# One-hot matrices of eight tokens in two VectorE instructions instead of four, residual loads and output gathers paced

## The chip, the cores and the metric

The kernel runs on one core of a Trainium2 chip. The metric is the device time of one execution in microseconds, here the median of three runs. TensorE multiplies 128x128 tiles, VectorE (DVE), ScalarE (ACT) and GpSimd (POOL) work on 128 partitions; SyncE (SP) and others issue DMAs.

## What is computed

Two layers of a trunk over 256 context rows and 512 latent rows of 1024 numbers. Each layer has a mixer (attention and a short convolution in layer 0, an mLSTM in layer 1) and then PEER, a layer of 16384 experts. PEER picks 16 experts for each token and each of 8 heads, and adds up their output rows:

```python
def block(xb):
    q = (xb @ w_q).reshape(PEER_BLOCK, PEER_HEADS, 2, PEER_DHALF)
    s = jnp.einsum('thpd,hpkd->thpk', q, subkeys).astype(jnp.float32)
    s1, i1 = lax.top_k(s[:, :, 0], PEER_TOPK)
    s2, i2 = lax.top_k(s[:, :, 1], PEER_TOPK)
    cand = (s1[..., :, None] + s2[..., None, :]).reshape(...)
    cidx = (i1[..., :, None] * PEER_NKEYS + i2[..., None, :]).reshape(...)
    top, pos = lax.top_k(cand, PEER_TOPK)
    idx = jnp.take_along_axis(cidx, pos, axis=-1)
    g = jax.nn.softmax(top, axis=-1)
    ue, ve = u[idx], v[idx]
    act = jax.nn.gelu(jnp.einsum('td,thkd->thk', xb, ue), approximate=False)
    return jnp.einsum('thk,thkd->td', g * act, ve)
```

The result is RMSNorm of the latent stream after layer 1.

## The kernel before

The span falls into stages: mixer of layer 0 (to about 485 us), peer_u of layer 0 (U0, to 1536), peer_v0 (V0, from 1579 to about 2290), mixer of layer 1 (to about 2670), peer_u of layer 1 (U1, to 3447), peer_v1 (V1, to the end).

Most blocks of 128 tokens ("dense" ones) don't gather expert rows. For them U multiplies all 16384 expert rows, 128 chunks of 128, by the tokens: a chunk is loaded (uf, L997), split into a high part by ScalarE (uh, L109) and a low part by VectorE (ul, L112), multiplied in three terms on TensorE (aps, L681), and put through Gelu by ScalarE (ga, L1024), which is stored to DRAM (gad). The routing weight of each expert pair is made as a matrix per token: over 128 (head, choice) pairs, a one-hot matrix of the first key index times a one-hot matrix of the second, the latter weighted by the softmax (in a high and a low part). V then multiplies gad by that weight (gf, read from gd) and by the output rows of all experts.

The one-hot matrices are made by `prep(t0)` for eight tokens: an iota tile is compared with the tokens' indices (L862 for the first index, L863 for the second), and the second is multiplied by the two parts of the weight (L865, twice). `gbuild(t0, g)` takes four of the eight tokens: for each, two matmuls of 128x128 (gps, L879), stationary from the first matrix, moving from the second; ScalarE copies the result to stg (L881), which is stored to gd. There are four dense blocks in U0 and three in U1, with 16 preps each.

The other blocks (two in layer 0, one in layer 1) are gathered by rows: POOL gathers urows (L922), VectorE takes a dot product (L928); in V, POOL gathers vrows (L1094) and VectorE adds them up (`v_add`: L1100, L1102).

What VectorE and TensorE do beside the chunks is laid out by a planner in peer_u: four queues (routing, the one-hot matrices with their matmuls, dot products, background work), each item with a weight in microseconds; in each chunk items are handed out until a share of the total weight is spent, from the queue that lags most. The scheduler of the language then orders the instructions of each engine; `tc.issue_after(x)` keeps what is in its block behind instruction x in the order. The gps matmuls stand on TensorE between the matmuls of the chunks.

In V, `v_chunk` loads a chunk of output rows (vf, L1063, on SP's queue), with gaf and gf (L1066, L1070), splits them and multiplies gaf by gf (L1083); TensorE adds up in acc (L1125 in V0, L1191 in V1), with matmuls that stand four chunks behind the loads. `finish` of V0 loads the residual rows vht (L1131) on POOL's queue; V1 loads fg (the last norm's gains, L1174, on SP's queue) and four vht (L1183, on POOL's) at its start.

Of the kernel before, what the change touches and what calls it, by code (L numbers as in the profile page):

```python
# [10 lines left out]
F32 = mybir.dt.float32  # L11
F32R = mybir.dt.float32r
F16 = mybir.dt.float16
# [3 lines left out]
ALU = mybir.AluOpType  # L17
# [4 lines left out]
P = 128  # L22
D = 1024
# [20 lines left out]
PH = 8  # L44
# [13 lines left out]
QS = 2  # L58
# [9 lines left out]
def row_bcast(ap, n):  # L68
    return bass.AP(tensor=ap.tensor, offset=ap.offset, ap=[[0, P], [1, n]])
# [3 lines left out]
def kernel(ctx: ExitStack, tc: tile.TileContext, a: dict, out: bass.AP, dbg=None, stop=None):  # L73
    nc = tc.nc
    dbg = dbg or {}
    vec, act, pe, pool = nc.vector, nc.scalar, nc.tensor, nc.gpsimd
# [575 lines left out]
    def peer_u(layer, tiles):  # L652
# [12 lines left out]
        with ExitStack() as s1:  # L665
# [101 lines left out]
            def stage2(t):  # L767
                H = 2 if t < ng else 4
                keep = t >= ng
                d = {}  # L770
# [81 lines left out]
                def prep(t0):  # L852
                    def f():
                        def col(q):
                            return d["it"][:, q, None, t0:t0 + 8].rearrange("p o (g t) -> p g o t", t=4) \
                                .to_broadcast([P, 2, P, 4])

                        io = GP[1][:, None].to_broadcast([P, 2, P, 4])
                        p1 = GP[0].tile([P, 2, P, 4], F16, name="p1", bufs=2)
                        p2 = [GP[0].tile([P, 2, P, 4], F16, name=f"p2{q}", bufs=2) for q in range(2)]  # L860
                        eq = GP[0].tile([P, 2, P, 4], F16, name="p2e", bufs=1)
                        vec.tensor_tensor(p1, io, col(0), op=ALU.is_equal)  # L862
                        vec.tensor_tensor(eq, io, col(1), op=ALU.is_equal)  # L863
                        for q in range(2):
                            vec.tensor_tensor(p2[q], eq, col(2 + q), op=ALU.mult)  # L865
                        d[t0] = p1, p2
                    return f

                def gbuild(t0, g):
                    def f():  # L870
                        t1 = t0 + 4 * g
                        o = t1 % 32
                        if o == 0:
                            d["stg"] = GP[0].tile([P, P, 32], F32, name="stg", bufs=2)
                        gp = pp.tile([P, 512], F32, name="gps", bufs=2)
                        p1, p2 = d[t0]
                        for i in range(4):
                            for q in range(2):
                                pe.matmul(gp[:, i * P:(i + 1) * P], p1[:, g, :, i], p2[q][:, g, :, i],  # L879
                                          start=q == 0, stop=q == 1)  # L880
                        act.mul(d["stg"][:, :, o:o + 4], gp.rearrange("p (t j) -> p j t", j=P), 1.0 / GSCALE)  # L881
                        if o == 28:
                            stores.extend((t - ng, t1 // 32, d["stg"], j) for j in range(0, P, P // GS))
                        elif stores and o % 8 == 0:
                            store()
                            if o == 24:
                                while stores:
                                    store()
                    return f
# [45 lines left out]
            GP = []  # L935

            def swap():
                sq.close()
                PK["gst"].close()
                gp = mkpool(PK["st"], f"gp{layer}", side="right")  # L940
                io = gp.tile([P, P, 4], F16, name="iota")
                pool.iota(io, pattern=[[1, P], [0, 4]], base=0, channel_multiplier=0,
                          allow_small_or_imprecise_dtypes=True)
                GP.extend((gp, io))

# [6 lines left out]
            one = heads[0]  # L952
            for t in range(ng, n):
                nxt = heads[t + 1 - ng] if t + 1 < n else []
                one.append((st2[t][2], 1.0, 0))
                for pf, g0, g1 in st2[t][3]:
                    one.append((pf, 2.75, 2 * PH * QS + 1))
                    for gf in (g0, g1):
                        pend.append(gf)
                        if len(pend) > 3:  # L960
                            one.append((pend.pop(0), 0.0, 0))
                        if nxt:
                            one.append(nxt.pop(0))
                one += nxt
# [46 lines left out]
            for c in range(128):  # L1011
# [17 lines left out]
                if c == 2 * PH * QS + 1:  # L1029
                    swap()  # L1030
# [11 lines left out]
                while True:  # L1042
# [3 lines left out]
                    q = max(ok, key=lambda q: lag(q, c))  # L1046
                    f, w, _ = queues[q].pop(0)
# [39 lines left out]
        return vh, vl, wh, wl  # L1087

    def v_add(y, n, vp, accs, fetched, VB):
        for x in range(VB) if y == 0 else (y + VB - 1,):  # L1090
            if x < n * P:
                i, k = x % n, x // n
                r = fetched[x] = vp.tile([P, D], F32, name="vrows", bufs=VB)
                nc.gpsimd.indirect_dma_start(  # L1094
                    out=r, out_offset=None, in_=a["v_t"].rearrange("l c k d -> (l c k) d"),
                    in_offset=bass.IndirectOffsetOnAxis(ap=GW["row"][i][:, k:k + 1], axis=0))
        i, k = y % n, y // n
        r, gw, acc = fetched.pop(y), GW["w"][i], accs[i]
        if k == 0:
            vec.tensor_scalar(acc, r, gw[:, 0:1], None, op0=ALU.mult)  # L1100
        else:
            vec.scalar_tensor_tensor(acc, r, gw[:, k:k + 1], acc, op0=ALU.mult, op1=ALU.add)  # L1102

    def peer_v0(gd, gad, src, dst):
        G = 4
        g, n = NG[0], NT - NG[0]
        TD = n * P
        with ExitStack() as st:
            ap_ = mkpool(RT["st"], "va0", side="right")
            vp = mkpool(st, "vp0")  # L1110
# [3 lines left out]
            state, fetched, chs, added = RT["state"], {}, {}, 0  # L1114
# [13 lines left out]
            def finish(t):  # L1128
                nonlocal last
                ht = ap_.tile([P, D], F32, name="vht", bufs=2)  # L1130
                nc.gpsimd.dma_start(ht, src[t])  # L1131
                gr = grow[1 if t < 2 else 0]
                if t < g:
                    vec.tensor_tensor(accs[t], accs[t], gr, op=ALU.mult)
                else:
                    for hf in range(2):
                        hs = slice(hf * 512, (hf + 1) * 512)
                        vec.tensor_tensor(accs[t][:, hs], acc[t - g][hf], gr[:, hs], op=ALU.mult)
                vec.tensor_tensor(accs[t], accs[t], ht, op=ALU.add)
                if t >= 2:  # L1140
                    nc.gpsimd.dma_start(dst[t], accs[t])
                rs = norm_stat(accs[t], vp, vp.tile([P, D], BF16, name="vjunk"))
                if last:
                    vec.tensor_scalar(accs[last[0]], accs[last[0]], last[1], None, op0=ALU.mult)
                last = (t, rs)
# [22 lines left out]
    def peer_v1(gd, gad, src):  # L1168
        G = 4
        with ExitStack() as st:  # L1170
            vp = mkpool(st, "vp1")
            pp = mkpsum(st, "vps1")
            fg = vp.tile([P, D], F32, name="fg")
            nc.sync.dma_start(fg, row_bcast(a["norm_f"], D))  # L1174
            acc = [[pp.tile([P, 512], F32, name=f"acc{i}_{hf}") for hf in range(2)] for i in range(3)]
            accg = vp.tile([P, D], F32, name="accg")
            fetched = {}
            TD = NLAT - P
            state = V1["state"]
            hts = []  # L1180
            for i in range(4):
                ht = vp.tile([P, D], F32, name=f"vht{i}")
                nc.gpsimd.dma_start(ht, src[2 + i])  # L1183
                hts.append(ht)

            def mm(c, i, ch):
                vh, vl, wh, wl = ch
# [14 lines left out]
                        v_add(k, 1, vp, [accg], fetched, VB1)  # L1202
            for c in range(128 - G + 1, 128):
                chs[c] = v_chunk(1, vp, vp, c, gd, gad, TD, state, G + 1, (VFB, GAB, 2))
            for i in range(-1, 3):
                ht = hts[i + 1]
                if i < 0:
                    parts = accg[:, :512], accg[:, 512:]
                else:
                    parts = acc[i]  # L1210
                    for c in range(128 - G, 128):
                        mm(c, i, chs[c])
                for hf in range(2):
                    hs = slice(hf * 512, (hf + 1) * 512)
                    tmp = vp.tile([P, 512], F32, name="vtmp", bufs=2)
                    vec.tensor_tensor(tmp, parts[hf], grow[0][:, hs], op=ALU.mult)
                    vec.tensor_tensor(ht[:, hs], ht[:, hs], tmp, op=ALU.add)
                ss = vp.tile([P, 1], F32, name="fss", bufs=2)
                junk = vp.tile([P, D], BF16, name="fjunk")
                act.activation(junk, ht, AF.Square, accum_out=ss)  # L1220
                rs = rstd(ss, vp, 1.0 / D)
                vec.scalar_tensor_tensor(ht, ht, rs, fg, op0=ALU.mult, op1=ALU.mult)
                nc.sync.dma_start(out[(i + 1) * P:(i + 2) * P, :], ht)
# [461 lines left out]
```

## Time and profile before

| | us |
|---|---|
| median of three runs (lowest to highest) | 3993.28 (3991.39 to 3998.4) |
| profiled execution | 4000.77 |
| its span | 3998.9 |
| TensorE busy | 3749.9 |
| VectorE busy | 3214.4 |
| ScalarE busy | 1502.1 |
| POOL busy | 1307.3 |

The mean granted clock of TensorE is 0.972 of full speed. The profile is of one execution, 7.5 us above the median; 1.9 us of its time lie outside the span. A busy share is an average over stages with different limits. PE is a matmul, PEld a weight load.

### The profile page before, as it was taken

What the parts mean: (1) busy time and instruction counts of PE and PEld (TensorE: products, weight loads), DVE (VectorE), ACT (ScalarE), POOL (GpSimd) and SP (SyncE); (2) the same over time, 40 slices, a digit from 0 to 9 for tenths busy, and PEclk for the clock granted to TensorE, in tenths of its full rate; (3) what the DMA queues carried; (4) which work ended last, traced back from release to release, by engine and by line L of the source; (5) the groups of instructions that cost most, each with busy time, mean ns of one, the idle gap of its engine ahead of it and who ended that gap; (6) DMA issues with size and microseconds to landing.
All of it is one profiled execution on the core that took longest, in us unless ns stands there. A gap on an engine that the chain in (4) does not pass through costs nothing. (4 is left out here: it accounts for less than half of the span.)

```text
span 3998.9 us, 54009 instructions
## 1 busy us (share of the span) xinstructions
PE 3749.9 (94%) x19201; PEld 3205.2 (80%) x19201; DVE 3214.4 (80%) x6734; ACT 1502.1 (38%) x2429; POOL 1307.3 (33%) x962
## 2 busy tenths in 40 slices
PE   6988899999999995999999899888999999899998
PEld 5776688887877774888888689777899999788887
DVE  7766599999989987888898854457988877688887
ACT  4355423334333332222223365543334343333333
POOL 1521203123443334766666312213112222332221
PEclk9999999999999997999999999989999999999999
DMA  7301366468999999999999721146558888899995
GB/s 245 103 6 45 134 200 224 162 203 293 332 334 338 378 360 360 388 391 389 389 390 389 259 65 44 38 165 221 183 165 278 305 300 301 320 388 355 360 360 210
DMA packets 411663, 1036.52 MB, mean 259 GB/s; under 512 B 35584, under 2 KB 170240, under 8 KB 411392
## 3 DMA queue, kind: packets, MB, share of 16 engines
q1 hardware_dynamic: 261920, 498.69, 35.8%
q0 software_dynamic: 114336, 416.34, 28.7%
q10 hardware_dynamic: 35136, 118.05, 7.6%
q8 instruction: 150, 2.46, 0.2%
q14 instruction: 121, 0.99, 0.1%
HBM read 906.05 MB, written 126.88 MB: 258 GB/s over the span
## 5 line engine op out<-in xcount | busy, mean ns | idle before, releaser
L922 POOL DMA_INDIRECT urows<-in_u_rows,urow x384 | 483.0, 1258 | 1348.0 <-DVE urows L928 697.9
L1094 POOL DMA_INDIRECT vrows<-in_v_t,vrow x384 | 600.5, 1564 | 582.7 <-DVE accg L1102 337.2
L681 PE MATMUL aps<-pnh,uh 128*128 128x512 f32 (+1 forms) x2048 | 769.8, 376 | 16.7 <-ACT ga L1024 12.4
L681 PE MATMUL aps<-pnh,ul 128*128 128x512 f32 (+1 forms) x2048 | 760.5, 371 | 0.1
L681 PE MATMUL aps<-pnl,uh 128*128 128x512 f32 (+1 forms) x2048 | 759.7, 371 | 0.0
L109 ACT CAST uh<-uf 128x1024 fp32r<-128x1024 f32 x256 | 269.2, 1052 | 756.3 <-PE aps L681 707.2
L928 DVE SCALAR_TENSOR_TENSOR urows<-urows,px 128x1024 f32<-128x1024 f32 x384 | 464.0, 1218 | 33.5 <-DMA urows<-in_u_rows,urow 33.5
L109 ACT CAST vh<-vf 128x1024 fp32r<-128x1024 f32 x255 | 268.0, 1052 | 534.3 <-issue 281.6
L681 PEld LDWEIGHTS aps<-pnh,uh 128*128 128x128 f32 x2048 | 391.2, 191 | 63.4 <-ACT ga L1024 16.0
L112 DVE TENSOR_TENSOR vl<-vf,vh 128x1024 fp32r<-128x1024 f32 x255 | 311.5, 1221 | 148.1 <-ACT vh L109 147.6
L681 PEld LDWEIGHTS aps<-pnh,ul 128*128 128x128 f32 x2048 | 389.7, 190 | 44.5 <-DVE ul L112 0.8
L681 PEld LDWEIGHTS aps<-pnl,uh 128*128 128x128 f32 x2048 | 390.2, 191 | 42.3
L112 DVE TENSOR_TENSOR ul<-uf,uh 128x1024 fp32r<-128x1024 f32 x256 | 312.3, 1220 | 103.8 <-ACT uh L109 103.2
L1125 PE MATMUL acc<-vh,vwh 128*128 128x512 f32 x1024 | 317.7, 392 | 48.0 <-ACT vwh L109 48.0
L1125 PE MATMUL acc<-vh,vwl 128*128 128x512 f32 x1024 | 317.1, 391 | 1.0 <-DVE vwl L112 0.7
L1125 PE MATMUL acc<-vl,vwh 128*128 128x512 f32 x1024 | 316.9, 391 | 0.0
L1102 DVE SCALAR_TENSOR_TENSOR vacc<-vrows,gw,vacc 128x1024 f32<-128x1024 f32 x254 | 313.9, 1277 | 0.0
L1125 PEld LDWEIGHTS acc<-vh,vwh 128*128 128x128 f32 x1024 | 192.6, 189 | 90.3 <-ACT vwh L109 50.5
L1191 PE MATMUL acc<-vh,vwh 128*128 128x512 f32 x768 | 239.3, 393 | 12.7 <-ACT vwh L109 12.1
L109 ACT CAST vwh<-gaf 128x512 fp32r<-128x512 f32 (+1 forms) x254 | 143.2, 564 | 283.7 <-DVE gaf L1083 153.8
L879 PE MATMUL gps<-p,p 128*128 128x128 f16 x1792 | 243.7, 297 | 3.3 <-DVE p L865 1.7
L1191 PE MATMUL acc<-vl,vwh 128*128 128x512 f32 x768 | 238.4, 392 | 0.0
(444 smaller groups left out, 7461.2 us busy)
## 6 DMA issues: line engine op xcount, KB each, us to landing
uf<-in_u_t SPq DMA_DIRECT2D x256, 512.0 KB
vf<-in_v_t SPq DMA_DIRECT2D x255, 512.0 KB
gd<-stg ACTq DMA_DIRECT2D x112, 512.0 KB
gf<-gd SPq DMA_DIRECT2D x220, 256.0 KB
wmt<-in_w_modT SPq DMA_DIRECT2D x90, 512.0 KB
gad<-ga ACTq DMA_DIRECT2D x64, 512.0 KB
gaf<-gad SPq DMA_DIRECT2D x63, 512.0 KB
gad<-ga ACTq DMA_DIRECT2D x64, 384.0 KB
```

Of the source, the lines that this page charges most:

```text
L109: act.copy(hi, src)
L112: return el.tensor_tensor(lo, src, hi.bitcast(F32), op=ALU.subtract)
L681: pe.matmul(ps[:, o:o + w], x[:, k, :], blk[q][:, k, :w], start=(k == 0 and x is wh and q == 0), stop=(k == KD - 1 and x is wl))
L879: pe.matmul(gp[:, i * P:(i + 1) * P], p1[:, g, :, i], p2[q][:, g, :, i], start=q == 0, stop=q == 1)
L922: nc.gpsimd.indirect_dma_start(out=r, out_offset=None, in_=a["u_rows"], in_offset=bass.IndirectOffsetOnAxis(ap=urow[j][:, k:k + 1], axis=0))
L928: vec.scalar_tensor_tensor(r, r, 1.0, PK["x"][j], op0=ALU.mult, op1=ALU.mult, accum_out=gact[j][:, k:k + 1])
L1094: nc.gpsimd.indirect_dma_start(out=r, out_offset=None, in_=a["v_t"].rearrange("l c k d -> (l c k) d"), in_offset=bass.IndirectOffsetOnAxis ...
L1102: vec.scalar_tensor_tensor(acc, r, gw[:, k:k + 1], acc, op0=ALU.mult, op1=ALU.add)
L1125: pe.matmul(acc[i][hf], x[:, ts_], y[:, hf * 512:(hf + 1) * 512], start=(c == 0 and first), stop=(c == 127 and end))
L1191: pe.matmul(acc[i][hf], x[:, ts_], y[:, hf * 512:(hf + 1) * 512], start=(c == 0 and first), stop=(c == 127 and last))
```

## The change

In `prep`, the two comparisons become one instruction of 128x2048 (tile `oh`, both matrices), and the two products become another (tile `p2`). Tokens stand innermost in eights instead of fours, so the matmuls of `gbuild` read columns that are 16 bytes apart instead of 8; the iota tile is twice as large. The planner's weight of a prep is 2.5 instead of 2.75. `v_add` gathers two rows per addition until VB rows are under way, instead of VB rows ahead of the first addition. The residual load in `finish` stands in `issue_after`. In V1 the loads of fg and of the four vht are written behind the last chunk's loads, in `issue_after`, and fg goes over POOL's queue.

```diff
@@ -852,18 +852,14 @@
                 def prep(t0):
                     def f():
                         def col(q):
-                            return d["it"][:, q, None, t0:t0 + 8].rearrange("p o (g t) -> p g o t", t=4) \
-                                .to_broadcast([P, 2, P, 4])
-
-                        io = GP[1][:, None].to_broadcast([P, 2, P, 4])
-                        p1 = GP[0].tile([P, 2, P, 4], F16, name="p1", bufs=2)
-                        p2 = [GP[0].tile([P, 2, P, 4], F16, name=f"p2{q}", bufs=2) for q in range(2)]
-                        eq = GP[0].tile([P, 2, P, 4], F16, name="p2e", bufs=1)
-                        vec.tensor_tensor(p1, io, col(0), op=ALU.is_equal)
-                        vec.tensor_tensor(eq, io, col(1), op=ALU.is_equal)
-                        for q in range(2):
-                            vec.tensor_tensor(p2[q], eq, col(2 + q), op=ALU.mult)
-                        d[t0] = p1, p2
+                            return d["it"][:, q:q + 2, None, t0:t0 + 8].to_broadcast([P, 2, P, 8])
+
+                        io = GP[1][:, None].to_broadcast([P, 2, P, 8])
+                        oh = GP[0].tile([P, 2, P, 8], F16, name="oh", bufs=2)
+                        p2 = GP[0].tile([P, 2, P, 8], F16, name="p2", bufs=2)
+                        vec.tensor_tensor(oh, io, col(0), op=ALU.is_equal)
+                        vec.tensor_tensor(p2, oh[:, 1, None].to_broadcast([P, 2, P, 8]), col(2), op=ALU.mult)
+                        d[t0] = oh[:, 0], p2
                     return f
 
                 def gbuild(t0, g):
@@ -876,7 +872,7 @@
                         p1, p2 = d[t0]
                         for i in range(4):
                             for q in range(2):
-                                pe.matmul(gp[:, i * P:(i + 1) * P], p1[:, g, :, i], p2[q][:, g, :, i],
+                                pe.matmul(gp[:, i * P:(i + 1) * P], p1[:, :, 4 * g + i], p2[:, q, :, 4 * g + i],
                                           start=q == 0, stop=q == 1)
                         act.mul(d["stg"][:, :, o:o + 4], gp.rearrange("p (t j) -> p j t", j=P), 1.0 / GSCALE)
                         if o == 28:
@@ -938,8 +934,8 @@
                 sq.close()
                 PK["gst"].close()
                 gp = mkpool(PK["st"], f"gp{layer}", side="right")
-                io = gp.tile([P, P, 4], F16, name="iota")
-                pool.iota(io, pattern=[[1, P], [0, 4]], base=0, channel_multiplier=0,
+                io = gp.tile([P, P, 8], F16, name="iota")
+                pool.iota(io, pattern=[[1, P], [0, 8]], base=0, channel_multiplier=0,
                           allow_small_or_imprecise_dtypes=True)
                 GP.extend((gp, io))
 
@@ -954,7 +950,7 @@
                 nxt = heads[t + 1 - ng] if t + 1 < n else []
                 one.append((st2[t][2], 1.0, 0))
                 for pf, g0, g1 in st2[t][3]:
-                    one.append((pf, 2.75, 2 * PH * QS + 1))
+                    one.append((pf, 2.5, 2 * PH * QS + 1))
                     for gf in (g0, g1):
                         pend.append(gf)
                         if len(pend) > 3:
@@ -1087,7 +1083,7 @@
         return vh, vl, wh, wl
 
     def v_add(y, n, vp, accs, fetched, VB):
-        for x in range(VB) if y == 0 else (y + VB - 1,):
+        for x in range(2) if y == 0 else range(min(2 * y, y + VB - 1), min(2 * y + 2, y + VB)):
             if x < n * P:
                 i, k = x % n, x // n
                 r = fetched[x] = vp.tile([P, D], F32, name="vrows", bufs=VB)
@@ -1128,7 +1124,8 @@
             def finish(t):
                 nonlocal last
                 ht = ap_.tile([P, D], F32, name="vht", bufs=2)
-                nc.gpsimd.dma_start(ht, src[t])
+                with tc.issue_after(state["lo"]):
+                    nc.gpsimd.dma_start(ht, src[t])
                 gr = grow[1 if t < 2 else 0]
                 if t < g:
                     vec.tensor_tensor(accs[t], accs[t], gr, op=ALU.mult)
@@ -1171,17 +1168,12 @@
             vp = mkpool(st, "vp1")
             pp = mkpsum(st, "vps1")
             fg = vp.tile([P, D], F32, name="fg")
-            nc.sync.dma_start(fg, row_bcast(a["norm_f"], D))
             acc = [[pp.tile([P, 512], F32, name=f"acc{i}_{hf}") for hf in range(2)] for i in range(3)]
             accg = vp.tile([P, D], F32, name="accg")
             fetched = {}
             TD = NLAT - P
             state = V1["state"]
             hts = []
-            for i in range(4):
-                ht = vp.tile([P, D], F32, name=f"vht{i}")
-                nc.gpsimd.dma_start(ht, src[2 + i])
-                hts.append(ht)
 
             def mm(c, i, ch):
                 vh, vl, wh, wl = ch
@@ -1202,6 +1194,12 @@
                         v_add(k, 1, vp, [accg], fetched, VB1)
             for c in range(128 - G + 1, 128):
                 chs[c] = v_chunk(1, vp, vp, c, gd, gad, TD, state, G + 1, (VFB, GAB, 2))
+            with tc.issue_after(state["lo"]):
+                nc.gpsimd.dma_start(fg, row_bcast(a["norm_f"], D))
+                for i in range(4):
+                    ht = vp.tile([P, D], F32, name=f"vht{i}")
+                    nc.gpsimd.dma_start(ht, src[2 + i])
+                    hts.append(ht)
             for i in range(-1, 3):
                 ht = hts[i + 1]
                 if i < 0:
```

VectorE in U1, at two neighbouring preps; p is a tile of one-hot matrices, p2e the one that is multiplied. Before:

```order
L863 TENSOR_TENSOR p2e<-iota,idT 128x1024 [waits DVE_49]
L865 TENSOR_TENSOR p_29845<-p2e,idT 128x1024 [waits DVE_49,PE_49]
L862 TENSOR_TENSOR p_29844<-iota,idT 128x1024 [waits PE_49]
L865 TENSOR_TENSOR p_29846<-p2e,idT 128x1024
L112 TENSOR_TENSOR ul<-uf,uh 128x1024 [waits DMAHW1_49,Activation_49]
L863 TENSOR_TENSOR p2e<-iota,idT 128x1024 [waits DVE_49]
L928 SCALAR_TENSOR_TENSOR urows,gact_23858<-urows,px_23264 128x1024 [waits DMASW0_49]
L865 TENSOR_TENSOR p_29910<-p2e,idT 128x1024 [waits DVE_49,PE_49]
```

After, at about the same place:

```order
L112 TENSOR_TENSOR ul<-uf,uh 128x1024 [waits DMAHW7_49,PE_49,Activation_49]
L924 SCALAR_TENSOR_TENSOR urows,gact_23602<-urows,px_23008 128x1024 [waits DMASW0_49]
L860 TENSOR_TENSOR oh<-iota,idT 128x2048 [waits PE_49]
L112 TENSOR_TENSOR ul<-uf,uh 128x1024 [waits DMAHW0_49,Activation_49]
L861 TENSOR_TENSOR p_29423<-oh,idT 128x2048 [waits DVE_49]
L860 TENSOR_TENSOR oh<-iota,idT 128x2048 [waits PE_49]
L112 TENSOR_TENSOR ul<-uf,uh 128x1024 [waits DMAHW2_49,Activation_49]
L861 TENSOR_TENSOR p_29521<-oh,idT 128x2048 [waits DVE_49]
```

Before, a prep's four instructions stand apart, with a split of u and a dot product between them; after, two instructions twice as long stand there, and the first of them waits for TensorE.

POOL at the end of U1 and the start of V1 (hd is the residual in DRAM; a wait for DMASW is for an earlier DMA of the queue, for DMAHW one of another queue). Before:

```order
L922 DMA urows<-in_u_rows,urow_23857 128x1024 [waits DMASW5_49,DVE_49]
L1183 DMA vht_31794<-hd_2_74 128x1024 [waits DMASW6_49,DVE_49,PE_49]
L1183 DMA vht_31796<-hd_3_75 128x1024 [waits DMASW7_49,DVE_49,PE_49]
L1183 DMA vht_31798<-hd_4_76 128x1024 [waits DMAHW3_49,DMAHW4_49,DMAHW2_49,DMAHW5_49,DMAHW1_49,DMAHW6_49,DMAHW0_49,DMAHW7_49,DMASW0_49,Activation_49]
L1183 DMA vht_31800<-hd_5_77 128x1024 [waits DMAHW3_49,DMAHW2_49,DMAHW5_49,DMAHW0_49,DMASW1_49]
L1094 DMA vrows<-in_v_t,vrow_23256 128x1024 [waits DMASW2_49]
L1094 DMA vrows<-in_v_t,vrow_23256 128x1024 [waits DMAHW3_49,DMAHW4_49,DMAHW2_49,DMAHW6_49,DMAHW1_49,DMAHW7_49,DMAHW0_49,DMASW3_49]
L1094 DMA vrows<-in_v_t,vrow_23256 128x1024 [waits DMASW4_49]
L1094 DMA vrows<-in_v_t,vrow_23256 128x1024 [waits DMASW5_49]
```

After, from the same place on:

```order
L1090 DMA vrows<-in_v_t,vrow_23000 128x1024 [waits DMASW6_49,DVE_49,Pool_49]
L1090 DMA vrows<-in_v_t,vrow_23000 128x1024 [waits DMAHW2_49,DMAHW3_49,DMAHW1_49,DMAHW4_49,DMAHW0_49,DMAHW5_49,DMASW7_49,DMAHW6_49,DVE_49,DMAHW7_49,PE_49,Activation_49]
L1090 DMA vrows<-in_v_t,vrow_23000 128x1024 [waits DMASW0_49]
L1090 DMA vrows<-in_v_t,vrow_23000 128x1024 [waits DMASW1_49]
L1090 DMA vrows<-in_v_t,vrow_23000 128x1024 [waits DMASW2_49]
L1090 DMA vrows<-in_v_t,vrow_23000 128x1024 [waits DMASW3_49]
L1090 DMA vrows<-in_v_t,vrow_23000 128x1024 [waits DMASW6_49,DMASW4_49,DVE_49]
L1198 DMA fg<-in_norm_f 128x1024 [waits DMASW5_49,PE_49,Activation_49]
L1090 DMA vrows<-in_v_t,vrow_23000 128x1024 [waits DMASW7_49,DVE_49]
L1201 DMA vht_35609<-hd_2_74 128x1024 [waits DMAHW5_49,DMAHW3_49,DMAHW7_49,DMAHW2_49,DMAHW0_49]
L1090 DMA vrows<-in_v_t,vrow_23000 128x1024 [waits DMASW0_49,DVE_49]
L1201 DMA vht_35611<-hd_3_75 128x1024 [waits DMASW1_49]
```

Seven gathers stand ahead of fg, and the loads of vht stand between later gathers, each of which waits for an addition on VectorE; before, the four vht stand ahead of all gathers. On POOL in V0 the loads of vht and the gathers stand in the same rows with the same waits, before and after. On SP, fg stood ahead of the first vf loads of V1 and is gone.

## Rows read from the trace of the kernel before

**Rows 1.** Page: busy time and share of the span, by engine, instructions.

```profile
PE 3749.9 (94%) x19201; PEld 3205.2 (80%) x19201; DVE 3214.4 (80%) x6734; ACT 1502.1 (38%) x2429; POOL 1307.3 (33%) x962
```

**Rows 2.** Windows: length, busy (instructions) by engine, granted clock, DMA share, GB/s.

```profile
900.00:1100.00 200.00, 199.91 (x998) 159.37 (x996) 183.86 (x424) 76.07 (x107) 75.43 (x61) 1.00 0.88 312
1100.00:1300.00 200.00, 196.03 (x971) 156.81 (x970) 185.62 (x370) 69.98 (x99) 78.45 (x63) 0.99 0.92 335
1300.00:1500.00 200.00, 190.43 (x1008) 150.82 (x1009) 182.34 (x297) 71.75 (x105) 72.14 (x57) 0.99 0.97 369
2990.00:3200.00 210.00, 210.00 (x1285) 206.17 (x1284) 183.60 (x388) 86.87 (x128) 49.17 (x41) 1.00 0.81 285
3200.00:3400.00 200.00, 200.00 (x1276) 194.84 (x1274) 155.41 (x231) 82.75 (x129) 45.08 (x41) 1.00 0.86 299
3460.00:3470.00 10.00, 10.00 (x37) 8.08 (x36) 7.56 (x10) 2.13 (x4) 3.61 (x3) 0.78 1.04 387
3470.00:3480.00 10.00, 5.50 (x22) 4.27 (x21) 2.32 (x4) 2.40 (x3) 0.00 (x0) 0.90 1.04 397
3500.00:3900.00 400.00, 400.00 (x1766) 331.36 (x1766) 334.11 (x398) 144.35 (x197) 111.61 (x103) 1.00 1.01 366
```

**Rows 3.** Groups by line and form: busy us, mean ns, idle before, releasers.

```profile
L112 DVE TENSOR_TENSOR ul<-uf,uh 128x1024 fp32r<-128x1024 f32 x256 | 312.3, 1220 | 103.8 <-ACT uh L109 103.2
...
L112 DVE TENSOR_TENSOR vwl<-gaf,vwh 128x512 fp32r<-128x512 f32 x126 | 86.0, 683 | 5.7 <-ACT vwh L109 5.7
...
L862 DVE TENSOR_TENSOR p<-iota,idT 128x1024 f16<-128x1024 f16 x112 | 76.7, 685 | 4.0 <-PE gps L879 4.0
```

**Rows 4.** One line, L865: durations ns, its waits, who waited for it.

```profile
L865 DVE TENSOR_TENSOR p<-p2e,idT x224: 659/685/695, 882.1 to 3427.2; 128x1024 f16<-128x1024 f16 x112
...
  PE gps L879: 52.1, 29
...
  PEld L879: 3.7, 5
```

**Rows 5.** Waits, 900 to 1500 us: who waits for whom, total us, times, longest.

```profile
ACT uh L109 <- PE aps L681: 208.9, 76, 5.5
...
PE aps L681 <- ACT ga L1024: 9.6, 7, 3.3
```

**Rows 6.** Chain that ended last, 3050 to 3058 us: start, us, what.

```profile
3054.97 1.90 PE gps L879 x16
```

**Rows 7.** One line, L879: weight loads, ns min/median/max, first and last start us.

```profile
L879 PEld LDWEIGHTS <-p x1792: 110/117/148, 905.6 to 3430.9; 128*128 128x128 f16 x200
```

**Rows 8.** Timeline of TensorE at 2703 us: start, us, instruction.

```profile
2703.18 0.27 PE L116 MATMUL tp<-skl,pqh 128*128 128x128 f32 x1
...
2704.30 0.27 PE L117 MATMUL tp<-skh,pql 128*128 128x128 f32 x1
2704.41 0.39 PE L681 MATMUL aps<-pnh,uh 128*128 128x384 f32 x1
```

**Rows 9.** Waits, 1530 to 1585 us, start of V0.

```profile
PE acc L1125 <- ACT vwh L109: 42.5, 1, 42.5
```

**Rows 10.** Chain, 3430 to 3500 us, start of V1.

```profile
3447.29 8.54 DMA gad<-ga
...
3457.48 19.66 DMA vf<-in_v_t
...
3478.67 21.55 PE acc L1191 x81
```

**Rows 11.** Waits, 3430 to 3490 us.

```profile
PE acc L1191 <- ACT vwh L109: 12.1, 2, 7.6
```

**Rows 12.** Timeline, 3442 to 3443 us.

```profile
3442.43 0.33 SPq L1174 DMA_DIRECT2D fg<-in_norm_f  x1
...
3442.87 0.58 POOL L1183 DMA_DIRECT2D vht<-hd  x1 [28.58 <-PE aps L681]
```

## Prediction

> **What bounds the kernel now.** I read the page first, then a table of windows over the stages that the change touches. Over the whole span TensorE is busy 94%, VectorE 80% [rows 1], so a cheaper VectorE instruction pays only where TensorE waits for VectorE. The change acts in four places: the build part of U0 (one-hot matrices, about 880 to 1531 us), that of U1 (2990 to 3431 us), the row additions of V0 and V1, and the first 40 us of V1.
>
> In the build part of U1 TensorE is busy 210.00 of 210 us and 200.00 of 200 us at a granted clock of 1.00, while VectorE has 26 and 45 us free [rows 2]. That stage is TensorE's. In U0, TensorE is busy 199.91, 196.03 and 190.43 us of three windows of 200 us [rows 2]: 13.6 us missing in 600, and VectorE (182 to 186 us of 200) has less than 10% free. So U0 is near balance, still on TensorE's side. At the start of V1, TensorE falls to 5.50 us of ten while the DMA share is 1.04 at 397 GB/s; later in V1 it is busy 400.00 of 400 us [rows 2]. So V1 starts on DMA and then runs on TensorE.
>
> **The one-hot matrices on VectorE.** One prep makes matrices of eight tokens. Before: four instructions of 128x1024 f16, each 685 ns [rows 3, 4], 2.74 us. After: two of 128x2048 f16. No row has that shape. A 128x512 f32 subtraction takes 683 ns, a 128x1024 one 1220 ns [rows 3]: doubling adds 537 ns. The f16 one of 1024 elements takes what 512 f32 take, so I take 1.22 us for 2048: 2.44 us a prep, 0.30 us less. Bounds: nothing saved (2 x 1.37 us) to these 0.30 us. There are 112 preps (L862 ran 112 times, [rows 3]): 64 in U0, 48 in U1, so at most 19 us and 14 us of VectorE time, 34 us in all.
>
> How much of that is on the path? In U1 nothing: VectorE's own wait ahead of L865 is for TensorE's gps matmuls, 52.1 us in 29 waits [rows 4]; a shorter prep makes that wait longer. The cover is VectorE's free time of 26 and 45 us per window, several times the 14 us. In U0 the direct measure is what TensorE waited for prep: its weight loads 3.7 us in 5 waits for L865 [rows 4]. Most of the 13.6 us missing has another cause: TensorE waits for ScalarE's ga (L1024), 9.6 us in 7 waits, and ScalarE in turn waits for TensorE before uh [rows 5]. So bounds for U0 are 0 and 13.6 us (19 if VectorE were the true pace-setter); nearest to the 3.7 us is **3 us**, since also the ul split behind a prep comes 0.3 us sooner. The planner's new weight (2.5 for 2.75) hands out 0.25 x 112 = 28 us less of booked work; items of the four queues move by some rows, at no cost that a row shows, since the sum of work is the same. The iota tile doubles: one POOL instruction per layer, ahead of the first prep; POOL is busy a third of the span [rows 1], so zero.
>
> **The same edit on TensorE.** The tokens' columns of a matrix stood 8 bytes apart in memory, and now 16 bytes apart, for the stationary and the moving operand of 1792 gps matmuls. Now: 16 of them take 1.90 us in the chain, 119 ns each [rows 6], and their weight loads have a median of 117 ns [rows 7]: the loads follow each other without a gap, and what a matmul itself needs lies beneath the next load, as I read it. Matmuls of the same 128x128 size with dense operands (scores against keys) start 112 ns apart: 11 from 2703.18 us to the next one's start at 2704.41, 1.23 us [rows 8]. So the step from dense to 8 bytes shows a cost of at most 7 ns. Price of the step to 16 bytes: the near end is zero, if weight loads keep 117 ns and streaming stays beneath them. A middle value is 148 ns, the longest weight load of this line [rows 7]: 148 - 119 = 29 ns, times 1792 is 52 us. The far end is that each column takes twice as long in both operands: 119 ns x 1792 = 213 us. All of it would be on the path, since TensorE has no time free in these stretches [rows 2]. A gain is excluded: the number and size of the matmuls are the same. I take **zero**, nearest to the row in which 8 bytes differ from dense by 7 ns, and keep the far end for a rival.
>
> [...] No run here shows a 16-byte step yet.
>
> **V0.** The order of POOL's rows shows residual loads and gathers of V0 at the same rows with the same waits as before: wrapped or not, the loads come where they came. Zero, for pacing and for the wrapped load. The 42.5 us that TensorE waits at V0's start for vwh [rows 9] stay: the last items of U0's queues are the same kind and number (dots and background rows; one prep, 0.3 us).
>
> **The start of V1.** The chain there goes: last ga store, 8.54 us to land; then gf on SP; then vf loads, which take 19.66 us until TensorE resumes [rows 10]; TensorE waits 12.1 us in two waits for vwh [rows 11]. In this stretch the queues are full, at 387 and 397 GB/s [rows 2]. Before, fg (0.5 MB) and four vht (2.0 MB) are issued from 3442.87 us on [rows 12], ahead of the gathers. 2.5 MB at some 390 GB/s are 6.4 us of full DMA. After, POOL issues seven gathers first, and then fg and the vht between further gathers, which wait for VectorE's additions. So the store of ga now meets three megabytes of gathers instead of two of vht, and the vf loads meet part of the 2.5 MB a few microseconds later: the bytes are moved behind, not far. SP loses one issue of 0.33 us ahead of vf [rows 12]. Bounds: the gain can't exceed the 12.1 us of waits; a loss can't easily exceed the 6.4 us of the moved bytes. I take half of the 6.4 us, **3 us** of gain. Behind this stretch V1 runs on TensorE with 366 GB/s, below the 397 that DMA reached, so bytes deferred further are hidden.
>
> **Sum.** 3 + 3 + 0 = 6 us less than the profiled 4000.77 us: 3994.8 us. The profiled execution was 7.5 us above the median of the runs, 3993.28; the difference carries over, so **3987 us**. About 8 us (0.2%) is what a measurement of this kernel tells from no change.
>
> **Rivals.**
> *More gain*: U0 is paced by VectorE after all. For it: VectorE's share there is 91 to 93%; against: only 3.7 us of TensorE's waits name prep. It gives 19 us, with V1's 6.4 us 25 us: 3968 us. Chance 0.08.
> *Slower, through the step of 16 bytes*: the price goes on top of the 6 us gained, at 1.79 us per nanosecond, so it decides from (6 + 8) / 1.79 = 8 ns a matmul on (119 to 127 ns). At 29 ns: 3987 + 52 = 4039 us, chance 0.12. At half to all of the far end (107 to 213 us): 4094 to 4200 us, chance 0.14. For it: both operands are touched, the cover of streaming beneath weight loads is unknown in size, and the loads themselves are the period. Against it: 8 bytes against dense shows only 7 ns. [...]
> *V1 loses*: vht and fg collide with vf loads that were clear before, 6.4 us lost and U0 gives nothing: 4000 us, within 0.2%; beyond it with chance 0.03.
> *Nothing changes*: V0's order is the same, U1 and the rest hide the VectorE time, V1 only shuffles bytes: 3993 us. This lies in the likeliest case's own range, 3975 to 4000 us, chance 0.63 for that range.
>
> **How the numbers follow.** Likeliest range 0.63, more gain 0.08, step of 16 bytes 0.26, V1's loss 0.03. Of the 0.63, faster by over 8 us (below 3985) takes 0.25, within 8 us 0.38. So faster 0.25 + 0.08 = 0.33, same 0.38, slower 0.26 + 0.03 = 0.29. The range goes from 3966 (more gain) to 4045 us (the 29 ns case); left out are the dearer step, 0.14, and 0.03 on the fast side.
>
> **What would show it.** Prep: two instructions of about 1.22 us at the new lines, or 1.37 us if nothing is saved. TensorE: the weight loads of gps stay at 117 ns and 16 of the matmuls take 1.9 us; were they above 2.03 us, the rival holds. U1's windows keep TensorE at 100% and VectorE's wait for gps grows. U0: missing TensorE time falls from 13.6 to about 10 us. V1: the two waits for vwh fall from 12.1 to about 9 us, and the first gather comes ahead of fg. What would make it wrong: longer gps matmuls, or U0's end moving by more than 10 us.

## The result

The changed kernel takes 4277.17 us (median of 4 runs, 4271.22 to 4285.96), the kernel before 3993.64 us: a ratio of 1.0703, 95% interval 1.069 to 1.0715. It is 283.5 us slower. I had forecast 3987 us, and a chance of 0.29 for slower.

The page after: busy time by engine, and the granted clock of TensorE in 40 slices.

```profile
PE 4049.7 (95%) x19201; PEld 3365.6 (79%) x19201; DVE 3204.0 (75%) x6510; ACT 1520.0 (35%) x2433; POOL 1365.9 (32%) x963
...
PEclk9999899999989988899999999899998988899999
```

TensorE is busy 300 us longer than in [rows 1], with the same 19201 matmuls; VectorE is 10 us shorter. The clock row has eights in U0 and U1. The windows of the build parts, with the same columns as [rows 2]:

```profile
900.00:1100.00 200.00, 200.00 (x814) 148.26 (x813) 150.65 (x307) 61.05 (x85) 67.00 (x48) 0.94 0.73 247
1100.00:1300.00 200.00, 198.79 (x804) 146.51 (x803) 147.17 (x260) 59.47 (x84) 76.29 (x52) 0.92 0.80 276
3300.00:3500.00 200.00, 200.00 (x984) 177.96 (x983) 134.37 (x242) 68.41 (x98) 44.07 (x34) 0.92 0.71 248
3500.00:3700.00 200.00, 200.00 (x921) 172.12 (x920) 111.90 (x133) 59.69 (x89) 38.67 (x31) 0.88 0.65 224
```

TensorE is still busy nearly all the time, so it is not waiting that made it slower: its work got longer, and the clock fell to between 0.88 and 0.94 in these windows, where it had been 0.99 to 1.00. VectorE has 49 to 88 us free per window. The two new instructions, by form, and then the line of the gps matmuls:

```profile
L860 DVE TENSOR_TENSOR oh<-iota,idT 128x2048 f16<-128x2048 f16 x112 | 137.0, 1223 | 161.9 <-PE gps L875 161.7
L861 DVE TENSOR_TENSOR p<-oh,idT 128x2048 f16<-128x2048 f16 x112 | 136.7, 1220 | 0.1
```

```profile
L875 PEld LDWEIGHTS <-oh x1792: 141/146/180, 910.8 to 3718.0; 128*128 128x128 f16 x200
...
  DVE oh L860: 161.7, 43
```

The two instructions take 1.22 us each, as predicted, and VectorE waits 161.7 us for gps, three times [rows 4]. But the weight loads went from 117 to 146 ns [rows 7], and the chain that ended last shows what the matmuls need:

```profile
3511.33 1.90 PE gps L875 x8
3513.24 0.18 PE aps L681
3513.41 1.90 PE gps L875 x8
3515.32 9.73 PE aps L681 x47
3525.05 3.77 PE gps L875 x16
3528.82 5.74 PE aps L681 x24
3534.55 3.77 PE gps L875 x16
3538.33 8.49 PE aps L681 x48
```

16 gps matmuls take 3.77 us, some 235 ns each, where [rows 6] has 1.90 us. The second thing to see is in the chunks (24 matmuls of L681 each, 4.25 us at the full clock, as in the 8.49 us for 48): behind two groups of 8 with a single matmul between them, 47 take 9.73 us, and behind the group of 16 at 3525.05 us a chunk takes 5.74 us. Not each group has this behind it: the next one, at 3534.55, has not. Windows of 4 us, with the clock as last figure but two:

```profile
3524.00:3528.00 4.00, 4.00 (x21) 2.72 (x20) 1.01 (x1) 2.04 (x3) 0.00 (x0) 1.00 0.98 376
3528.00:3532.00 4.00, 4.00 (x17) 3.81 (x16) 4.00 (x6) 0.60 (x1) 0.10 (x1) 0.66 0.75 266
```

The group of 16 begins at 3525 us, and the clock of its window is 1.00. In the next window the mean is 0.66. In windows of 0.5 us the clock is 1.00 up to 3529.0 us, 0.50 in each from 3529.5 to 3532.5 us, and 1.00 again from 3533.0 us, so about two thirds of the window with 0.66 is at 0.50 and the rest at 1.00. So the change has two prices on TensorE: 112 x (3.77 - 1.90) = 209 us for the groups, and the remaining 74 us, which I read as chunks behind them at the lower clock; e9 and e12 test that.

At the start of V1, TensorE's waits are these:

```profile
PE acc L1183 <- ACT vwh L109: 5.5, 2, 4.5
...
PE acc L1183 <- ACT ga L1020: 5.2, 1, 5.2
```

That is 10.7 us in three waits. The kernel before has, beside the two waits of [rows 11], this one:

```profile
PE acc L1191 <- ACT ga L1024: 0.6, 1, 0.6
```

So it had 12.7 us in three waits. On POOL, fg and the first vht come late: fg stands behind the seven gathers that the order shows, and an eighth stands ahead of the first vht.

```profile
3749.87 0.59 POOL L1198 DMA_DIRECT2D fg<-in_norm_f  x1
...
3754.77 0.60 POOL L1201 DMA_DIRECT2D vht<-hd  x1
```

### The profile page after: what moved, and what is told of

Same layout as the page of the kernel before. It is cut to its first block, busy times and chain, and to the rows that moved or that the text cites. A ratio compares the mean times of both kernels' runs of the same rounds, so it can differ in the third digit from the quotient of the medians.

```text
span 4283.8 us, 53762 instructions
## 1 busy us (share of the span) xinstructions
PE 4049.7 (95%) x19201; PEld 3365.6 (79%) x19201; DVE 3204.0 (75%) x6510; ACT 1520.0 (35%) x2433; POOL 1365.9 (32%) x963
## 5 line engine op out<-in xcount | busy, mean ns | idle before, releaser
L918 POOL DMA_INDIRECT urows<-in_u_rows,urow x384 | 527.1, 1373 | 1577.7 <-DVE urows L924 908.2
L681 PE MATMUL aps<-pnh,uh 128*128 128x512 f32 (+1 forms) x2048 | 815.6, 398 | 7.5 <-ACT ga L1020 4.4
L681 PE MATMUL aps<-pnl,uh 128*128 128x512 f32 (+1 forms) x2048 | 799.1, 390 | 0.0
L681 PE MATMUL aps<-pnh,ul 128*128 128x512 f32 (+1 forms) x2048 | 798.6, 390 | 0.0
L681 PEld LDWEIGHTS aps<-pnh,uh 128*128 128x128 f32 x2048 | 419.4, 205 | 66.3 <-ACT ga L1020 5.9
L681 PEld LDWEIGHTS aps<-pnl,uh 128*128 128x128 f32 x2048 | 418.3, 204 | 51.7
L681 PEld LDWEIGHTS aps<-pnh,ul 128*128 128x128 f32 x2048 | 417.2, 204 | 52.3
L875 PE MATMUL gps<-p,oh 128*128 128x128 f16 x1792 | 444.3, 414 | 0.0
L875 PEld LDWEIGHTS <-oh 128*128 128x128 f16 x1792 | 249.9, 147 | 159.2 <-issue 26.5
L1121 PE MATMUL acc<-vh,vwh 128*128 128x512 f32 x1024 | 318.0, 392 | 44.1 <-ACT vwh L109 44.1
L1121 PE MATMUL acc<-vl,vwh 128*128 128x512 f32 x1024 | 316.8, 391 | 0.0
L860 DVE TENSOR_TENSOR oh<-iota,idT 128x2048 f16<-128x2048 f16 x112 | 137.0, 1223 | 161.9 <-PE gps L875 161.7
L877 ACT ACTIVATE stg<-gps 128x512 f32<-128x512 f32 x224 | 134.3, 600 | 340.3 <-PE gps L875 335.5
```

What stands on the lines that cost most here:

```text
L681: pe.matmul(ps[:, o:o + w], x[:, k, :], blk[q][:, k, :w], start=(k == 0 and x is wh and q == 0), stop=(k == KD - 1 and x is wl))
L860: vec.tensor_tensor(oh, io, col(0), op=ALU.is_equal)
L875: pe.matmul(gp[:, i * P:(i + 1) * P], p1[:, :, 4 * g + i], p2[:, q, :, 4 * g + i], start=q == 0, stop=q == 1)
L918: nc.gpsimd.indirect_dma_start(out=r, out_offset=None, in_=a["u_rows"], in_offset=bass.IndirectOffsetOnAxis(ap=urow[j][:, k:k + 1], axis=0))
L1121: pe.matmul(acc[i][hf], x[:, ts_], y[:, hf * 512:(hf + 1) * 512], start=(c == 0 and first), stop=(c == 127 and end))
```

## The experiments

All ratios are to the kernel before on the same chip, with 95% intervals.

**Two instructions, 8-byte columns** (e1), the changed kernel with the tokens in fours; the two indices and the two weight parts stand side by side in `it`, so that one instruction reads both:

```diff
-oh = GP[0].tile([P, 2, P, 8], F16, name="oh", bufs=2)
+oh = GP[0].tile([P, 4, P, 4], F16, name="oh", bufs=2)
...
-pe.matmul(..., p1[:, :, 4 * g + i], p2[:, q, :, 4 * g + i], ...)
+pe.matmul(..., p1[:, g, :, i], p2[:, 2 * q + g, :, i], ...)
```

> The changed kernel with its two 2048-element instructions kept, but the tokens laid out in fours again, so that the gps matmuls read columns 8 bytes apart. Theory A (the 16-byte step is the cost): gps matmuls back at 117 to 119 ns from start to start, granted clock back at 1.00 in U1, total 3980 to 3995 us. Rival C (the cost lies in the two long VectorE instructions or in the moved loads): the period stays above 200 ns or TensorE waits for prep, total above 4200 us.

Measured: 3987.8 us, ratio 0.9973 (0.9962 to 0.9984). The weight loads, and a piece of the chain in U1:

```profile
L879 PEld LDWEIGHTS <-oh x1792: 111/117/166, 910.6 to 3426.0; 128*128 128x128 f16 x200
```

```profile
3053.63 1.90 PE gps L879 x16
```

The loads are back at 117 ns [rows 7], and 16 matmuls at 1.90 us [rows 6]. With the step alone undone all of the loss is gone. Rival C falls.

**Four instructions, 16-byte columns** (e2), the kernel before with the layout alone:

```diff
-p1 = GP[0].tile([P, 2, P, 4], F16, name="p1", bufs=2)
+p1 = GP[0].tile([P, P, 8], F16, name="p1", bufs=2)
...
-pe.matmul(..., p1[:, g, :, i], p2[q][:, g, :, i], ...)
+pe.matmul(..., p1[:, :, 4 * g + i], p2[q][:, :, 4 * g + i], ...)
```

> The kernel before with nothing changed but the layout: four instructions of 1024 elements as before, tokens in eights, columns 16 bytes apart. Theory A: gps period about 235 ns, 16 of them 3.77 us, 1792 x 118 ns = 211 us more, and a further 70 to 80 us in which the chunk behind each group of 16 runs at a lower granted clock: 4265 to 4290 us. Rival C: 3985 to 4000 us.

Measured: 4282.14 us, ratio 1.0714 (1.0696 to 1.0732). A piece of the chain in U1:

```profile
3301.31 3.77 PE gps L878 x16
3305.08 5.72 PE aps L681 x24
```

The step alone makes all of the loss, with both of its prices.

**One operand each** (e3: `p2` in eights and `p1` in fours; e4: the other way round):

```diff
+pe.matmul(..., p1[:, g, :, i], p2[q][:, :, 4 * g + i], ...)   # e3
+pe.matmul(..., p1[:, :, 4 * g + i], p2[q][:, g, :, i], ...)   # e4
```

> The kernel before with only the moving operand of gps 16 bytes apart, the stationary one still 8. Theory A1 (the moving operand's reads set the period): about 235 ns, total 4260 to 4290 us, weight loads 117 ns. Rival A2 (the weight load sets it): 118 ns, total 3985 to 4000 us.

> The kernel before with only the stationary operand of gps 16 bytes apart, the moving one still 8. Theory A1: weight loads go from 117 to 147 ns and are the period, 1792 x 29 ns = 52 us more, total 4040 to 4060 us, more if the clock falls too. Rival A2 (the weight load sets the 235 ns): 4260 to 4290 us.

Measured: e3 4268.56 us, ratio 1.0677 (1.0656 to 1.0698); e4 4009.64 us, ratio 1.0029 (1.0019 to 1.0039). The weight loads of e3 and a piece of its chain:

```profile
L883 PEld LDWEIGHTS <-p x1792: 110/118/147, 903.1 to 3698.0; 128*128 128x128 f16 x200
```

```profile
3205.35 3.69 PE gps L883 x16
3209.05 4.24 PE aps L681 x24
```

The weight loads are as before, and 16 matmuls take 3.69 us, 231 ns each. The same two views of e4:

```profile
L883 PEld LDWEIGHTS <-p x1792: 140/145/173, 907.8 to 3445.5; 128*128 128x128 f16 x200
```

```profile
3178.95 1.99 PE gps L883 x16
```

Here the weight loads take 145 ns, and yet 16 matmuls take 1.99 us, 124 ns each. So the moving operand sets the pace; a weight load of 145 ns mostly lies beside other work. A1 was right on e3. For e4 it had the load of 147 ns as the period, and that was wrong: the loads got that long, but they did not become the period, and 11 us were lost instead of 52.

**The loads and the pacing alone** (e5): prep, gbuild, iota and weight as before.

> The changed kernel with prep, gbuild, iota and the planner's weight as before, so that only the loads and the pacing in V0 and V1 are changed. If these carry the 0.27% that the kernel with two instructions and 8-byte columns gains: ratio 0.996 to 0.9985, V1 shorter by 2 to 10 us. If the VectorE time of prep carries it: ratio 0.999 to 1.001, and the gain is found in U0.

Measured: 3993.68 us, ratio 0.9995 (0.9985 to 1.0004). This is no gain that the total can tell.

**The two instructions alone** (e10), with 8-byte columns and the weight of 2.5:

> The kernel before with the two 2048-element instructions and the planner's weight of 2.5 alone, 8-byte columns, V0 and V1 as before. If VectorE's time of prep is what gained 0.27% beside the changed loads: ratio 0.996 to 0.9985, U0's build part 5 to 10 us shorter. If both parts were needed or it was neither: 0.999 to 1.001.

Measured: 3995.3 us, ratio 0.9993 (0.9984 to 1.0002). Neither part alone shows the 0.27% of e1. The product of the two ratios is 0.9988, and with the intervals of both it can't be told from e1's ratio, which was measured on another chip. I leave open whether the parts need each other. The traces, one of each kernel, say something on the loads that the totals don't: from the last gps matmul of U1 to the end of the span, the kernels with the moved loads (the changed one, e1, e5, e6, e7, e12) take 560 to 566 us, and those without (before, e2, e3, e4, e9, e10, e13) 566 to 569 us.

**Dense columns** (e6) and **4-byte columns** (e7), two instructions each, otherwise the changed kernel:

```diff
+oh = GP[0].tile([P, 2, 8, P], F16, name="oh", bufs=2)   # e6, each token's 128 columns together
+oh = GP[0].tile([P, 8, P, 2], F16, name="oh", bufs=2)   # e7, tokens in twos; `it` as in e1
```

> The changed kernel with each token's one-hot column block written densely (2-byte step) for both operands, still two instructions of 2048 elements. Theory A1 (the moving operand's reads set the period, 118 ns at 8 bytes, 231 at 16): the period falls until another limit is met, to 60 to 80 ns, 16 matmuls in 1.0 to 1.3 us, 70 to 100 us of TensorE time less; the total then hangs on VectorE, which reads one token's value for 128 elements: if its instruction stays at 1.22 us, 3890 to 3930 us; if it takes 2.3 us, U0 becomes VectorE's and the total is 3950 to 4060 us. Rival (the period has a floor near 112 ns, as dense f32 matmuls of this size have): 3980 to 3995 us with 1.22 us.

> The same with tokens in twos (4-byte step). Theory A1: the period falls below 118 ns, to 60 to 90 ns; VectorE's instruction stays at 1.22 us if pairs of two-byte values are enough for its speed; total 3890 to 3950 us. Rival (floor near 112 ns): 3980 to 3995 us.

Measured: e6 4086.18 us, ratio 1.0222 (1.0206 to 1.0237); e7 **3918.02 us, ratio 0.9818** (0.9795 to 0.9841). A piece of e7's chain, VectorE's instruction, and a window in U0:

```profile
3201.28 0.93 PE gps L879 x16
3202.21 4.22 PE aps L681 x24
```

```profile
L863 DVE TENSOR_TENSOR oh<-iota,idT 128x2048 f16<-128x2048 f16 x112 | 136.6, 1220 | 30.2 <-PE gps L879 30.1
```

```profile
900.00:1100.00 200.00, 187.70 (x1009) 148.06 (x1008) 188.66 (x404) 73.14 (x106) 95.70 (x66) 0.99 0.90 328
```

16 matmuls in 0.93 us, 58 ns each: half of the 8-byte time. In this window of U0 TensorE now has 12 us of 200 free, and VectorE 11, so part of what TensorE saves there isn't won. In e6: TensorE's timeline, the weight loads, VectorE's instruction by form, and a window in U0:

```profile
1002.81 1.07 PE L875 MATMUL gps<-p,oh 128*128 128x128 f16 x16
1003.69 0.48 PE L681 MATMUL aps<-pnh,ul 128*128 128x512 f32 x1
```

```profile
L875 PEld LDWEIGHTS <-oh x1792: 95/98/204, 906.5 to 3524.1; 128*128 128x128 f16 x200
```

```profile
L861 DVE TENSOR_TENSOR p<-oh,idT 128x2048 f16<-128x2048 f16 x112 | 255.8, 2284 | 0.0
```

```profile
1100.00:1300.00 200.00, 171.29 (x845) 131.11 (x844) 196.50 (x309) 59.67 (x87) 110.56 (x58) 0.92 0.86 300
```

From 1002.81 to 1003.69 us 16 matmuls start, 55 ns each. VectorE takes 2284 ns for the instruction with 128 equal values side by side, and is busy 196.50 of 200 us while TensorE is busy 171.29: VectorE's stage, as expected for that price, though 26 us slower than the range said.

**4-byte columns alone** (e13), on the kernel before, without the other edits:

> The kernel before with two instructions of 2048 elements, 4-byte columns and the planner's weight of 2.5, V0 and V1 as before. gps period 57 ns as in the run with the changed loads; if those loads add nothing: ratio 0.980 to 0.984; if they cost or bring something, the difference to 0.9818 shows it.

Measured: 3921.76 us, ratio 0.9813 (0.98 to 0.9827). This is e7's gain; the totals can't tell what the moved loads add to it. In the traces the stretch behind the last gps matmul takes 566 us in e13 and 560 in e7.

**The clock: twice the matmuls at 8 bytes** (e9), and **the groups of 16 broken up** (e12):

```diff
-for q in range(2):
-    pe.matmul(..., p1[:, g, :, i], p2[q][:, g, :, i], start=q == 0, stop=q == 1)
+for q in range(4):   # e9, and the scale halved
+    pe.matmul(..., p1[:, g, :, i], p2[q % 2][:, g, :, i], start=q == 0, stop=q == 3)
...
+if k == KD // 2 and late:   # e12, in proj: a group of 8 that was held back comes here
+    at_, gf = late.pop(0)
+    with tc.issue_after(at_):
+        gf()
```

> The kernel before with 8-byte columns, each gps matmul issued twice and the sum halved: groups of 32 matmuls of 118 ns last as long as groups of 16 of 235 ns, with twice the columns. It adds 1792 x 118 ns = 211 us. Theory D1 (the clock falls behind a group because its columns come slowly): the granted clock stays at 1.00 behind the groups, 24 matmuls of a chunk take 4.25 us, total 4195 to 4220 us. Rival D2 (it falls because a group of any gps matmuls lasts 3.8 us): the chunk behind a group takes 5.7 us, total 4260 to 4290 us.

> The changed kernel with every second group of 8 gps matmuls put into the middle of the next chunk's matmuls: 51 groups of 16 stand together instead of 94, the number and step of the matmuls are as in the changed kernel. Theory D1 (slow columns for 3.8 us without a break, then a lower clock): the 75 to 80 us that are lost beside the longer matmuls shrink with the groups of 16, to some 42 us, total 4235 to 4255 us. Rival D3 (the share of slow columns over the stage sets the clock): 4270 to 4285 us.

Measured: e9 4156.38 us, ratio 1.0393 (1.0377 to 1.0409); e12 4237.72 us, ratio 1.0599 (1.058 to 1.0618). The chain of e9:

```profile
3152.65 3.80 PE gps L879 x32
3156.44 4.24 PE aps L681 x24
```

A group lasts 3.80 us, as long as in the changed kernel, but the chunk behind it takes 4.24 us. The chain of e12 in U1:

```profile
3518.80 1.90 PE gps L881 x8
3520.70 2.09 PE aps L685 x12
```

Here are groups of 8 at 238 ns a matmul, each followed by half a chunk in 2.1 us, the full clock's time. The build parts of U0 and of U1 as whole windows, about from the first to the last gps matmul, with the clock as last figure but two, for the changed kernel, e9 and e12 in turn:

```profile
911.00:1690.00 779.00, 777.41 (x3111) 573.92 (x3110) 571.74 (x1002) 228.01 (x322) 279.89 (x191) 0.92 0.79 275
3160.00:3715.00 555.00, 555.00 (x2652) 485.91 (x2651) 345.21 (x532) 179.82 (x263) 111.93 (x90) 0.90 0.66 228
```

```profile
898.00:1599.00 701.00, 700.12 (x4001) 593.03 (x3999) 584.58 (x1139) 221.14 (x311) 254.45 (x197) 1.00 0.87 309
3068.00:3583.00 515.00, 515.00 (x3413) 504.27 (x3412) 354.60 (x637) 183.06 (x267) 102.74 (x87) 1.00 0.74 244
```

```profile
910.00:1689.00 779.00, 775.22 (x3112) 570.83 (x3111) 573.42 (x998) 226.31 (x320) 284.26 (x193) 0.92 0.80 275
3159.00:3673.00 514.00, 514.00 (x2657) 441.95 (x2656) 344.36 (x518) 179.54 (x264) 110.49 (x90) 1.00 0.71 246
```

In the traces the changed kernel has 91 groups of 16 (the expectation says 94) and e12 has 51. They were not broken up evenly: U0 goes from 52 to 49, U1 from 39 to 2. So U0 is a control: it keeps its groups, its clock of 0.92 and its 779 us, while U1 gets back to a clock of 1.00 and is 41 us shorter, which is the whole of the 39 us by which e12 is faster than the changed kernel. In e12, U1 has as many slow matmuls as in the changed kernel, at a clock of 1.00, so D3 falls. In e9 the groups last as long with faster matmuls, at 1.00 in both parts, so D2 falls. In the build parts of the changed kernel's trace the clock dropped to 0.50 62 times within 1 us of the end of one of the 91 groups of 16 slow matmuls, and in U1 behind two of the three pairs of groups of 8 that have only one matmul of a chunk between them (9.73 us for 47 matmuls, above); with half a chunk between them, in U1 of e12, it stayed at 1.00. What the chip itself looks at when it lowers the clock is not shown. In U0 the groups were not broken up in any run; there e9's clock of 1.00 is the evidence.

e9 is 39 us below its range for other reasons. TensorE's free time in U0's build part, 13.6 us before [rows 2], is 0.9 us, and the wait at V0's start, 42.5 us [rows 9], became

```profile
PE acc L1125 <- ACT vwh L109: 9.9, 2, 5.3
```

because in e9's order nothing stands on VectorE behind the last split of u, where the kernel before has some 29 rows (14 dot products, 7 of background work). That the wait is shorter for this reason is argued, not tried by itself.

## Why the prediction was wrong, by its steps

*VectorE* was right: 1.22 us per instruction. That it is hidden in U1 behind a longer wait for gps is seen in e1, where the columns are 8 bytes apart: VectorE waits there 63.9 us for gps, where it was 52.1 + 4.0 = 56.1 us before [rows 3, 4]. Most of the changed kernel's 161.7 us come from the slower gps. The 3 us that I took for U0 are too few to be told from nothing by e10's total (0.9984 to 1.0002). *V0 unchanged* and *V1 a few microseconds* agree with the runs: TensorE's waits at V1's start fell by 2.0 us where I took 3, and the stretch behind U1 is some microseconds shorter in each trace with the moved loads; e5's total (0.9985 to 1.0004) can't tell 3 us from nothing.

The step that failed is "I take **zero**, nearest to the row in which 8 bytes differ from dense by 7 ns". The cost was 112 x (3.77 - 1.90) = 209 us, close to my far end of 213 us, which belonged to the rival that I gave 0.14. Two readings were behind it. First, "what a matmul itself needs lies beneath the next load": e3 and e4 show the reverse, the moving operand sets the pace. For the same reason my middle value was no price: with loads of 145 ns e4 lost 11 us, not 52. Second, the row I took for dense was the wrong one. The 112 ns of [rows 8] are not the time of 128 dense columns: e6 has dense f16 columns at 55 ns, and for the f32 of [rows 8] itself the trace of before has, a few rows on in the same timeline,

```profile
2704.81 0.33 PE L681 MATMUL aps<-pnh,ul 128*128 128x384 f32 x1
2704.98 0.34 PE L681 MATMUL aps<-pnh,uh 128*128 128x384 f32 x1
2705.16 0.33 PE L681 MATMUL aps<-pnl,uh 128*128 128x384 f32 x1
```

384 dense columns start 0.17 to 0.18 us apart, 0.46 ns a column, where gps needed 119 / 128 = 0.93 ns. That could have told me that the step of 8 bytes already cost half of TensorE's speed. That the next doubling would cost as much again could not be read from it; e2 and e3 show it.

The rival itself lacked a term: the clock. By its far end it gave 4200 us; the other 74 us of the loss are the chunks at the lower clock, which e9 and e12 tell apart from the slower matmuls.

## What to carry to other kernels

Look at the step between the columns that a matmul reads as moving operand, and take nanoseconds per column from the start-to-start time of a long matmul (0.46 ns a column here, over 384 columns), not of a short one whose pace something else may set (112 / 128 = 0.88 ns in [rows 8]). For two-byte data, pairs of tokens (4 bytes) kept VectorE's instruction at 1.22 us and TensorE's matmul at 58 ns, near the 55 ns of dense columns. Dense columns nearly doubled VectorE's time, to 2.28 us, and eights (16 bytes) took 235 ns on TensorE, four times the 58 ns. Before a VectorE saving is bought with a layout, ask which engine reads that layout next, and whether that engine is the bound.

## What was not expected of the hardware

The gps matmul's time against the step of the moving operand: 55 ns at 2 bytes, 58 at 4, 119 at 8, 231 to 235 at 16. Why the step costs this is not shown. The weight load's: 98 ns at 2 bytes, 117 at 8, 145 at 16, mostly beside other work. The granted clock was 0.66 in the window of 4 us that takes in the end of a group of 16 matmuls of 235 ns and the chunk behind it, and 0.90 and 0.92 over the build parts with such groups. It was 1.00 over those with groups of 32 matmuls of 119 ns, and over U1 with the slow matmuls in groups of 8.
